# Column means of an 8192 × 8192 matrix: longer load runs, and three slabs folded on TensorE instead of one

## The chip, the cores and the metric

The kernel runs on one core of a Trainium2 chip. The metric is the device time of the kernel in microseconds, the median of several runs. One execution was also taken with the hardware profiler; its "span" runs from its first to its last instruction.

## The reference

```python
x = np.random.randn(8192, 8192).astype(np.float32)
def reference(x):
    return np.mean(x, axis=0)
```

So 268.4 MB are read, each element is added once into one of 8192 column sums, and 8192 floats are written.

## The kernel before

A **slab** is 128 rows, one row on each of the 128 partitions of the on-chip memory (SBUF); in float32 a slab is 4.19 MB and one row 32 KB. There are 64 slabs. They are loaded mostly two at a time, a **pair**: a partition gets two rows, 16384 elements, in one of three buffers `bufs[0..2]` (L48). Since a column sum doesn't depend on which row lands on which partition, rows are handed out so that each partition reads long contiguous runs of memory: `blocks` (L73) gives each partition RUN = 7 consecutive rows per block, so that a partition's rows start 7 × 32 KB = 224 KB after those of the partition before it. `source` (L78) takes three pairs from each block, as runs of 64 KB, and the seventh rows that are left over (`single`, L75) make pairs 27 to 30 and slab 62, as runs of 32 KB at most. The last slab, 63, is the last 128 rows of `x`, a partition's row 32 KB after that of the partition before.

`cuts` (L85) says into how many loads a pair is split: pair 0 into two (its first 2048 columns, then the rest), pairs 1 to 24 into one, pairs 25 to 29 into two rows of 8192 columns, pair 30 into four half rows. Slab 62 comes in two halves (L161), the last slab in eight pieces (L165): four wide ones of 2048, 2048, 2048 and 1408 columns, and four narrow ones of 192, 288, 96 and 64. All loads but pair 0's are issued by SyncE (SP) in this order, and SP's queue is in order: a load that waits holds up those behind it. The load of pair k waits until pair k − 3's buffer is free, which is when VectorE (DVE) has done the first add of pair k − 2 (L149 to L151); slab 62 and the pieces of the last slab share the buffer of pair 28 and wait in the same way, for the first add of pair 29 (L162).

**DVE** does nearly all of the summing. With the running sum in the first half of one buffer, each pair takes two adds of 8192 columns: `new[0:C] += old[0:C]` (frees the old buffer), then `new[0:C] += new[C:2C]`. Pairs 1 to 24 are done in a loop of eight turns (L181, LOOPED = 24), the others by a written-out list `adds` (L116 to L134), one add for each load, each waiting for its own load: two adds per pair for 25 to 29, four adds of 4096 columns for pair 30, and four of 2048 columns that add slab 62 to the running sum, `total`.

**TensorE (PE)** sums over the partitions: a matmul with a 128 × 32 matrix of ones as the stationary operand adds up 128 partitions of up to 512 columns into a bank of PSUM. `fold_wide` (L207) does a wide piece with four such matmuls, one to each quarter of the array's columns; `fold_narrow` (L215) does a narrow piece with one. Each matmul is two records in the trace, so a wide fold is eight. PE folds `total` piece by piece as DVE finishes it (`open_wide`, L234), and each piece of the last slab on top of it as that lands (`close`, L226), in an order written out at L239 to L256. Ahead of that, it does four matmuls on an unused tile `idle` (L240).

**The end**: ScalarE (ACT) drains wide pieces 0 to 2 from PSUM, times 1/8192, DVE drains wide piece 3, and both share the narrow ones (`drain`, L263). Four stores follow, three on SP and the last on ACT (L314 to L319).

Of the kernel before, what the change touches and what calls it, by code (L numbers as in the profile page):

```python
# [7 lines left out]
F32 = mybir.dt.float32  # L8
ADD = mybir.AluOpType.add
MULT = mybir.AluOpType.mult  # L10
P = 128
# [3 lines left out]
WIDE = (2048, 2048, 2048, 1408)  # L15
NARROW = (192, 288, 96, 64)
PIECES = WIDE + NARROW
FIRST = 2048
BY_ROW = 6
RUN = 7  # L20
LOOPED = 24


@with_exitstack
def kernel(
# [5 lines left out]
    nc = tc.nc  # L31
    R, C = x.shape
    n_slabs = R // P
    n_pairs = n_slabs // 2 - 1
    N0 = sum(WIDE)
    H = C // 2
    assert n_slabs % 2 == 0 and N0 + sum(NARROW) == sum(PIECES) == C
    assert LOOPED % 3 == 0 and LOOPED < n_pairs - 1
    inv_r = 1.0 / float(R)

    const_pool = ctx.enter_context(tc.tile_pool(name="const", bufs=1))
    psum_pool = ctx.enter_context(
        tc.tile_pool(name="acc", bufs=1, space=bass.MemoryType.PSUM)
    )
    res_pool = ctx.enter_context(tc.tile_pool(name="res", bufs=1))

    ones = const_pool.tile([P, 32], F32, name="ones")
    bufs = [nc.alloc_sbuf_tensor(f"pair{b}", [P, 2 * C], F32, align_bytes=512).ap() for b in range(3)]  # L48
    banks = [psum_pool.tile([P, 512], F32, name=f"bank{b}", tag=f"bank{b}") for b in range(8)]
    rw = nc.alloc_sbuf_tensor("rw", [P, 3 * 512], F32).ap()  # L50
    r3 = nc.alloc_sbuf_tensor("r3", [P, WIDE[3] // GROUPS], F32).ap()
    row = nc.alloc_sbuf_tensor("row", [P, C - N0], F32).ap()[0:1, :]
    idle = res_pool.tile([P, 512], F32, name="idle")

    wide, lo = [], 0
    for n, w in enumerate(WIDE):
# [2 lines left out]
    narrow = []  # L59
    for n, w in enumerate(NARROW):  # L60

        at = NARROW[2] if n == 3 else 0
        narrow.append((lo, w, 32 * min(n, 2), banks[4 + min(n, 2)], at))
        lo += w
    ending = (narrow[2][0], sum(NARROW[2:]), narrow[2][2], narrow[2][3], 0)

    n_blocks = (R - P) // (P * RUN)
    n_whole = n_blocks * (RUN // 2)  # L70
    assert R == (n_blocks * RUN + 1) * P and 2 * n_whole + n_blocks == 2 * n_pairs + 1
    assert LOOPED < n_whole
    blocks = x[0 : R - P, :].rearrange("(b p j) c -> b p (j c)", p=P, j=RUN)  # L73

    def single(n, lo, hi):  # L75
        return blocks[n, :, (RUN - 1) * C + lo : (RUN - 1) * C + hi]

    def source(k, lo, hi):  # L78
        if k < n_whole:
            b, t = divmod(k, RUN // 2)  # L80
            return blocks[b, :, 2 * t * C + lo : 2 * t * C + hi]
        j = lo // C
        return single(2 * (k - n_whole) + j, lo - j * C, hi - j * C)

    def cuts(k):  # L85
        if k == 0:
            return [(0, FIRST), (FIRST, 2 * C)]
        if k < n_pairs - BY_ROW:
            return [(0, 2 * C)]
        step = H if k == n_pairs - 1 else C  # L90
        return [(lo, lo + step) for lo in range(0, 2 * C, step)]

    def untracked(ap, size):

# [5 lines left out]


    early = nc.scalar.dma_start(out=untracked(bufs[0][:, 0:FIRST], 2 * C * P), in_=source(0, 0, FIRST))  # L102
    early.then_inc(first, 16)
    tc.no_tile_sem_insts.add(early.ins.name)
# [4 lines left out]
    with tc.tile_critical(sync_engine=mybir.EngineType.Pool) as section:  # L109
        tc.declare_no_dep(section, early.ins, reason="awaited by first")  # L110
        freed, half = sem("freed"), sem("half")
        dve, act, pe = sem("dve"), sem("act"), sem("pe")
        came = {}


        adds, freed_by = [], {}  # L116
        for k in range(LOOPED + 1, n_pairs):
            pair, before = bufs[k % 3], bufs[(k - 1) % 3]
            pieces = cuts(k)
            for n, (lo, hi) in enumerate(pieces):  # L120
                if lo < C:
                    adds.append(((k, n), pair[:, lo:hi], before[:, lo:hi]))
                else:
                    adds.append(((k, n), pair[:, lo - C : hi - C], pair[:, lo:hi]))
                if hi == C:
                    freed_by[k - 1] = len(adds)
        total = bufs[(n_pairs - 1) % 3]
        slab = bufs[n_pairs % 3][:, 0:C]
        last = bufs[n_pairs % 3][:, C : 2 * C]
        parts = [(lo, lo + 2048) for lo in range(0, C, 2048)]  # L130
        done = []
        for lo, hi in parts:
            adds.append((("slab", lo // H), total[:, lo:hi], slab[:, lo:hi]))
            done.append(len(adds))  # L134


        def load(key, dst, src, after=None):

            ld = (nc.scalar if key[0] == 0 else nc.sync).dma_start(out=dst, in_=src)  # L139
            if after is not None:  # L140
                ld.wait_op(after[0], after[1], "sem-ge")
            if key not in came:
                came[key] = sem(f"came_{'_'.join(map(str, key))}")
            ld.then_inc(came[key], 16)

        for k in range(n_pairs):
            for n, (lo, hi) in enumerate(cuts(k)):
                after = None
                if k >= 3 and n == 0:  # L149
                    f = k - 3  # L150
                    after = (freed, f + 1) if f < LOOPED else (dve, freed_by[f])  # L151
                if k == 1:
                    after = (first, 16)
                key = (k, n)
                if k <= LOOPED:
                    came[key] = first if (k, n) == (0, 0) else landed[k % 3]
                if key == (0, 0):
                    continue
                load(key, bufs[k % 3][:, lo:hi], source(k, lo, hi), after)
        r = (n_slabs - 2) * P  # L160
        for n in range(2):  # L161
            after = (dve, freed_by[n_pairs - 3]) if n == 0 else None  # L162
            load(("slab", n), slab[:, n * H : n * H + H], single(n_blocks - 1, n * H, n * H + H), after)
        at, lo = {}, 0
        for n, w in enumerate(PIECES):  # L165
            load(("last", n), last[:, lo : lo + w], x[r + P : R, lo : lo + w])
            for c in range(lo, lo + w, 32):
                at[c] = came["last", n]
            lo += w


# [1 line left out]
            return nc.vector.tensor_tensor(out=a, in0=a, in1=b, op=ADD)  # L173

        nc.vector.memset(ones, 1.0)  # L175
        nc.vector.memset(idle, 0.0)  # L176
        nc.vector.wait_ge(first, 16)
        vadd(bufs[0][:, 0:C], bufs[0][:, C : 2 * C]).wait_op(landed[0], 16, "sem-ge").then_inc(landed[0], -16)
        with nc.vector.register("left") as left:
            nc.vector.reg_mov(left, LOOPED // 3)  # L180
            with nc.vector.While(lambda: nc.vector.snap(left) > 0):  # L181
# [22 lines left out]
        def mm(dst, src, **flags):  # L204
            return nc.tensor.matmul(out=dst, lhsT=ones, rhs=src, skip_group_check=True, **flags)  # L205

        def fold_wide(n, src, **flags):  # L207
            lo, w, bank = wide[n]
            q = w // GROUPS
            for g in range(GROUPS):  # L210
                a = lo + g * q
                m = mm(bank[32 * g : 32 * g + 32, 0:q], src[:, a : a + q], **flags)
            return m

        def fold_narrow(part, src, **flags):  # L215
            lo, w, g, bank, at = part
            return mm(bank[g : g + 32, at : at + w], src[:, lo : lo + w], **flags)
# [3 lines left out]
        def landed_at(lo):  # L221
            if at[lo].num not in waited:
                waited.add(at[lo].num)
                nc.tensor.wait_ge(at[lo], 16)

        def close(fold, n, lo):  # L226
            nonlocal n_pe
            landed_at(lo)
            fold(n, last, start=False, stop=n != narrow[2]).then_inc(pe, 1)
            n_pe += 1  # L230
            return n_pe

        ready = {}
        def open_wide(n):  # L234
            nc.tensor.wait_ge(dve, done[n])
            fold_wide(n, total, start=True, stop=False)


        nc.tensor.wait_ge(dve, done[0] - 2)  # L239
        for _ in range(4):  # L240
            nc.tensor.matmul(  # L241
                out=banks[7][:, 0:512], lhsT=idle[:, 0:P], rhs=idle, start=True, stop=True, skip_group_check=True
            )
        open_wide(0)
        open_wide(1)
        ready["wide", 0] = close(fold_wide, 0, wide[0][0])
        open_wide(2)
        ready["wide", 1] = close(fold_wide, 1, wide[1][0])
        nc.tensor.wait_ge(dve, done[3])
        fold_wide(3, total, start=True, stop=False)  # L250
        for part in (*narrow[:2], ending):
            fold_narrow(part, total, start=True, stop=False)
        ready["wide", 2] = close(fold_wide, 2, wide[2][0])
        ready["wide", 3] = close(fold_wide, 3, wide[3][0])
        for n in range(len(narrow)):
            ready["narrow", n] = close(fold_narrow, narrow[n], narrow[n][0])  # L256

# [19 lines left out]
        for n, (engine, part) in enumerate(  # L277
            ((nc.scalar, narrow[0]), (nc.vector, narrow[1]), (nc.scalar, ending))
        ):
            lo, w, g, bank, _ = part  # L280
# [69 lines left out]
```

## Time and profile before

| what | value |
|---|---|
| median of 3 runs | 627.12 us (626.93 to 627.29) |
| the profiled execution, and its span | 627.51 us, 625.7 us |
| PE busy | 13.6 us, 86 matmul records |
| DVE busy | 541.3 us, 71 instructions |
| ACT busy | 3.7 us |
| HBM read over the span | 268.44 MB, 429 GB/s |
| DVE add of 8192 / 4096 / 2048 columns | 8.69 / 4.42 / 2.29 us, ×59 / ×4 / ×4 |
| PE: matmul records of 512 / 352 columns with `ones` | ×48 / ×16 |
| loads issued by SP | 48 |
| a whole pair's load, from issue to landing | 29.8 us (median of 24) |

How to read the profile: the page's slices cut the span into 40 equal parts of 15.6 us and show each engine's busy share in tenths, the TensorE clock granted, and what the 16 DMA engines moved. The chain of waits starts at the last instruction and goes back at each step to what released it; here it is read in order of time, one line per step, with start and duration in us, and "issue" for time in which nothing that the profile shows was waited for. The timeline has one line per stretch of like instructions (start, duration, engine, line, operation, output and input, count), with the idle time before it and its releaser in brackets. SPq and ACTq are the queues of DMA issues, PEld the loads of PE's stationary operand. L173 is every DVE add, L205 every matmul with `ones`, L139 every load.

### The profile page before, as it was taken

What the parts mean: (1) busy time and instruction counts of PE and PEld (TensorE: products, weight loads), DVE (VectorE), ACT (ScalarE), POOL (GpSimd) and SP (SyncE); (2) the same over time, 40 slices, a digit from 0 to 9 for tenths busy, and PEclk for the clock granted to TensorE, in tenths of its full rate; (3) what the DMA queues carried; (4) which work ended last, traced back from release to release, by engine and by line L of the source; (5) the groups of instructions that cost most, each with busy time, mean ns of one, the idle gap of its engine ahead of it and who ended that gap; (6) DMA issues with size and microseconds to landing.
All of it is one profiled execution on the core that took longest, in us unless ns stands there. A gap on an engine that the chain in (4) does not pass through costs nothing.

```text
span 625.7 us, 475 instructions
## 1 busy us (share of the span) xinstructions
PE 13.6 (2%) x86; PEld 4.6 (1%) x86; DVE 541.3 (87%) x71; ACT 3.7 (1%) x6; POOL 0.2 (0%) x4
## 2 busy tenths in 40 slices
PE   0000000000000000000000000000000000000025
PEld 0000000000000000000000000000000000000011
DVE  0049999989888899888898888988889899999996
ACT  0000000000000000000000000000000000000001
POOL 0000000000000000000000000000000000000000
PEclk9999999999999999999999999999999999999999
DMA  9999999999999999999999999999999999999997
GB/s 377 436 461 402 469 402 469 402 469 402 469 402 469 402 432 440 402 469 402 469 402 469 402 469 402 469 402 469 402 465 406 432 425 419 434 436 436 434 422 320
DMA packets 7231, 268.48 MB, mean 429 GB/s; under 512 B 1069, under 2 KB 1329, under 8 KB 1470
## 3 DMA queue, kind: packets, MB, share of 16 engines
q1 hardware_dynamic: 6940, 260.08, 96.2%
q10 hardware_dynamic: 290, 8.39, 3.2%
q14 instruction: 1, 0.01, 0.0%
HBM read 268.44 MB, written 0.03 MB: 429 GB/s over the span
## 4 chain that ended last, share of the span: by engine, by line
DMA 59%; DVE 39%; issue 0%; SPq 0%; DVEq 0%; PE 0%; ACTq 0%
DMA pair<-in_x_dram 59%; DVE pair L173 39%; SPq L139 0%; PE bank L205 0%; DVE r L269 0%; DVEq L109 0%; ACTq L102 0%; DVEq L186 0%; DVEq L184 0%; DVEq L173 0%; ACTq L345 0%
## 5 line engine op out<-in xcount | busy, mean ns | idle before, releaser
L173 DVE TENSOR_TENSOR pair<-pair 128x8192 f32<-128x8192 f32 (+2 forms) x67 | 539.7, 8056 | 78.0 <-DMA pair<-in_x_dram 73.7
L241 PE MATMUL bank<-idle 128*128 128x512 f32 x8 | 5.3, 817 | 605.6 <-DVE pair L173 605.6
L205 PE MATMUL bank<-pair,ones 128*32 128x512 f32 (+5 forms) x78 | 8.4, 523 | 3.8 <-DVE pair L173 3.6
L241 PEld LDWEIGHTS bank<-idle 128*128 128x128 f32 x8 | 2.1, 276 | 607.9 <-DVE pair L173 605.6
L266 ACT ACTIVATE rw<-bank 128x512 f32<-128x512 f32 x3 | 1.8, 597 | 617.3 <-PE bank L205 617.3
L269 DVE TENSOR_SCALAR r<-bank 128x352 f32<-128x352 f32 x1 | 0.5, 525 | 3.2 <-PE bank L205 3.2
L205 PEld LDWEIGHTS bank<-pair,ones 128*32 128x32 f32 x78 | 2.5, 108 | 10.2 <-DVE pair L173 7.1
L266 ACT ACT_TABLE_LOAD x1 | 1.3, 1283 | 1.8 <-issue 1.8
L175 DVE MEMSET ones<- 128x32 f32 x1 | 0.1, 85 | 1.0 <-PEq L334 1.0
L266 ACT ACTIVATE row<-bank 1x192 f32<-1x192 f32 (+1 forms) x2 | 0.6, 308 | 0.7 <-PE bank L205 0.7
L176 DVE MEMSET idle<- 128x512 f32 x1 | 0.5, 485 | 0.1
L269 DVE TENSOR_SCALAR row<-bank 1x288 f32<-1x288 f32 x1 | 0.4, 448 | 0.0
L334 POOL MEMSET const-bfloat16-1.0<- 128x1 bf16 x1 | 0.1, 101 | 0.0
L334 POOL MEMSET const-uint8-127<- 128x1 uint8 x1 | 0.1, 101 | 0.0
L334 POOL MEMSET const-float32-0.0<- 128x1 f32 x1 | 0.1, 98 | 0.2 <-issue 0.2
L334 POOL MEMSET const-float32-1.0<- 128x1 f32 x1 | 0.1, 98 | 0.0
## 6 DMA issues: line engine op xcount, KB each, us to landing
pair<-in_x_dram SPq DMA_DIRECT2D x10, 4096.0 KB, 27.6
pair<-in_x_dram SPq DMA_DIRECT2D x6, 2048.0 KB, 28.4
pair<-in_x_dram ACTq DMA_DIRECT2D x1, 7168.0 KB, 37.9
pair<-in_x_dram SPq DMA_DIRECT2D x3, 1024.0 KB, 33.4
pair<-in_x_dram ACTq DMA_DIRECT2D x1, 1024.0 KB, 4.7
pair<-in_x_dram SPq DMA_DIRECT2D x1, 704.0 KB, 36.6
pair<-in_x_dram SPq DMA_DIRECT2D x24, 29.8
pair<-in_x_dram SPq DMA_DIRECT2D x1, 144.0 KB, 30.2
```

Of the source, the lines that this page charges most:

```text
L173: return nc.vector.tensor_tensor(out=a, in0=a, in1=b, op=ADD)
L175: nc.vector.memset(ones, 1.0)
L176: nc.vector.memset(idle, 0.0)
L205: return nc.tensor.matmul(out=dst, lhsT=ones, rhs=src, skip_group_check=True, **flags)
L241: nc.tensor.matmul(out=banks[7][:, 0:512], lhsT=idle[:, 0:P], rhs=idle, start=True, stop=True, skip_group_check=True)
L266: op = engine.mul(out=dst, in_=src, mul=inv_r).then_inc(act, 1)
L269: op = engine.tensor_scalar(out=dst, in0=src, scalar1=inv_r, scalar2=None, op0=MULT).then_inc(dve, 1)
L334: nc = _bacc.Bacc("TRN2", target_bir_lowering=False, num_devices=1)
```

## The change

RUN becomes 6: a block gives each partition six consecutive rows, 192 KB apart from partition to partition, and three pairs in 64 KB runs with no row left over. Ten blocks make pairs 0 to 29; pair 30 is the next 256 rows (`two`), and slab 62 and the last slab together are the final 256 rows (`end`), two consecutive rows to a partition, so 64 KB apart. Every pair but pair 0 is one load. Slab 62 and the first 2048 columns of the last slab lie side by side both in memory and in the buffer, and come in one load of 40 KB runs; the other seven pieces of the last slab are loaded as before. DVE's loop covers 27 pairs; pairs 28 and 29 are written out. Pair 30 isn't added to the running sum any more: DVE adds its two slabs to each other, 2048 columns at a time. PE folds four things into each bank: the running sum, pair 30's sum, slab 62, and the last slab. The four matmuls on `idle` and the tile itself are gone.

```diff
-BY_ROW = 6
-RUN = 7
-LOOPED = 24
+RUN = 6
+LOOPED = 27
...
+    per_block = RUN // 2
+    n_blocks = (n_pairs - 1) // per_block
+    R0 = n_blocks * RUN * P
+    blocks = x[0:R0, :].rearrange("(b p j) c -> b p (j c)", p=P, j=RUN)
+    two = x[R0 : R0 + 2 * P, :].rearrange("(p j) c -> p (j c)", j=2)
+    end = x[R0 + 2 * P : R, :].rearrange("(p j) c -> p (j c)", j=2)
...
     def source(k, lo, hi):
-        if k < n_whole:
-            b, t = divmod(k, RUN // 2)
-            return blocks[b, :, 2 * t * C + lo : 2 * t * C + hi]
-        j = lo // C
-        return single(2 * (k - n_whole) + j, lo - j * C, hi - j * C)
+        if k == n_pairs - 1:
+            return two[:, lo:hi]
+        b, t = divmod(k, per_block)
+        return blocks[b, :, 2 * t * C + lo : 2 * t * C + hi]
 
     def cuts(k):
-        if k == 0:
-            return [(0, FIRST), (FIRST, 2 * C)]
-        if k < n_pairs - BY_ROW:
-            return [(0, 2 * C)]
-        step = H if k == n_pairs - 1 else C
-        return [(lo, lo + step) for lo in range(0, 2 * C, step)]
+        return [(0, FIRST), (FIRST, 2 * C)] if k == 0 else [(0, 2 * C)]
...
+        for k in range(LOOPED + 1, n_pairs - 1):
             pair, before = bufs[k % 3], bufs[(k - 1) % 3]
+            adds.append(((k, 0), pair[:, 0:C], before[:, 0:C]))
+            freed_by[k - 1] = len(adds)
+            adds.append(((k, 0), pair[:, 0:C], pair[:, C : 2 * C]))
+        n_total = len(adds)
+        total = bufs[(n_pairs - 2) % 3]
+        pair = bufs[(n_pairs - 1) % 3]
...
-            adds.append((("slab", lo // H), total[:, lo:hi], slab[:, lo:hi]))
+            adds.append(((n_pairs - 1, 0), pair[:, lo : lo + 2048], pair[:, C + lo : C + lo + 2048]))
             done.append(len(adds))
...
+        final = bufs[n_pairs % 3]
+        load(("slab", 0), final[:, 0 : C + WIDE[0]], end[:, 0 : C + WIDE[0]], (dve, freed_by[n_pairs - 3]))
         for n, w in enumerate(PIECES):
+            key = ("last", n) if n else ("slab", 0)
+            if n:
+                load(key, final[:, C + lo : C + lo + w], end[:, C + lo : C + lo + w])
...
+        def fold_all(src, **flags):
+            for n in range(len(wide)):
+                fold_wide(n, src, **flags)
+            for part in (*narrow[:2], ending):
+                fold_narrow(part, src, **flags)
+
+        nc.tensor.wait_ge(dve, n_total)
+        fold_all(total, start=True, stop=False)
+        for n in range(len(wide)):
             nc.tensor.wait_ge(dve, done[n])
-            fold_wide(n, total, start=True, stop=False)
...
+            fold_wide(n, pair, start=False, stop=False)
         for part in (*narrow[:2], ending):
+            fold_narrow(part, pair, start=False, stop=False)
+        landed_at(0)
+        fold_all(slab, start=False, stop=False)
+        for n in range(len(wide)):
+            ready["wide", n] = close(fold_wide, n, wide[n][0])
         for n in range(len(narrow)):
             ready["narrow", n] = close(fold_narrow, narrow[n], narrow[n][0])
```

More of the change, by code (lines that the diff above doesn't have):

```diff
@@ L35 @@
     N0 = sum(WIDE)
-    H = C // 2
     assert n_slabs % 2 == 0 and N0 + sum(NARROW) == sum(PIECES) == C
-    assert LOOPED % 3 == 0 and LOOPED < n_pairs - 1
+    assert LOOPED % 3 == 0 and LOOPED < n_pairs - 2
     inv_r = 1.0 / float(R)
@@ L44 @@
     )
-    res_pool = ctx.enter_context(tc.tile_pool(name="res", bufs=1))
     ones = const_pool.tile([P, 32], F32, name="ones")
@@ L52 @@
     row = nc.alloc_sbuf_tensor("row", [P, C - N0], F32).ap()[0:1, :]
-    idle = res_pool.tile([P, 512], F32, name="idle")
     wide, lo = [], 0
@@ L65 @@
     ending = (narrow[2][0], sum(NARROW[2:]), narrow[2][2], narrow[2][3], 0)
[L69 to L76, printed above, removed]
-    def source(k, lo, hi):
-        if k < n_whole:
-            b, t = divmod(k, RUN // 2)
-            return blocks[b, :, 2 * t * C + lo : 2 * t * C + hi]
-        j = lo // C
-        return single(2 * (k - n_whole) + j, lo - j * C, hi - j * C)
-    def cuts(k):
-        if k == 0:
-            return [(0, FIRST), (FIRST, 2 * C)]
-        if k < n_pairs - BY_ROW:
-            return [(0, 2 * C)]
-        step = H if k == n_pairs - 1 else C
-        return [(lo, lo + step) for lo in range(0, 2 * C, step)]
+    per_block = RUN // 2
+    n_blocks = (n_pairs - 1) // per_block
+    R0 = n_blocks * RUN * P
+    assert n_blocks * per_block == n_pairs - 1 and R == R0 + 4 * P
+    blocks = x[0:R0, :].rearrange("(b p j) c -> b p (j c)", p=P, j=RUN)
+    two = x[R0 : R0 + 2 * P, :].rearrange("(p j) c -> p (j c)", j=2)
+    end = x[R0 + 2 * P : R, :].rearrange("(p j) c -> p (j c)", j=2)
+    def source(k, lo, hi):
+        if k == n_pairs - 1:
+            return two[:, lo:hi]
+        b, t = divmod(k, per_block)
+        return blocks[b, :, 2 * t * C + lo : 2 * t * C + hi]
+    def cuts(k):
+        return [(0, FIRST), (FIRST, 2 * C)] if k == 0 else [(0, 2 * C)]
     def untracked(ap, size):
@@ L116 @@
         adds, freed_by = [], {}
-        for k in range(LOOPED + 1, n_pairs):
+        for k in range(LOOPED + 1, n_pairs - 1):
             pair, before = bufs[k % 3], bufs[(k - 1) % 3]
[L119 to L127, printed above, removed]
+            adds.append(((k, 0), pair[:, 0:C], before[:, 0:C]))
[4 more added lines that the diff above has]
+        pair = bufs[(n_pairs - 1) % 3]
         slab = bufs[n_pairs % 3][:, 0:C]
         last = bufs[n_pairs % 3][:, C : 2 * C]
-        parts = [(lo, lo + 2048) for lo in range(0, C, 2048)]
         done = []
-        for lo, hi in parts:
-            adds.append((("slab", lo // H), total[:, lo:hi], slab[:, lo:hi]))
+        for lo in range(0, C, 2048):
+            adds.append(((n_pairs - 1, 0), pair[:, lo : lo + 2048], pair[:, C + lo : C + lo + 2048]))
             done.append(len(adds))
@@ L159 @@
                 load(key, bufs[k % 3][:, lo:hi], source(k, lo, hi), after)
[L160 to L163, printed above, removed]
+        final = bufs[n_pairs % 3]
+        load(("slab", 0), final[:, 0 : C + WIDE[0]], end[:, 0 : C + WIDE[0]], (dve, freed_by[n_pairs - 3]))
         at, lo = {}, 0
         for n, w in enumerate(PIECES):
-            load(("last", n), last[:, lo : lo + w], x[r + P : R, lo : lo + w])
+            key = ("last", n) if n else ("slab", 0)
+            if n:
+                load(key, final[:, C + lo : C + lo + w], end[:, C + lo : C + lo + w])
             for c in range(lo, lo + w, 32):
-                at[c] = came["last", n]
+                at[c] = came[key]
             lo += w
@@ L175 @@
         nc.vector.memset(ones, 1.0)
-        nc.vector.memset(idle, 0.0)
         nc.vector.wait_ge(first, 16)
@@ L233 @@
         ready = {}
-        def open_wide(n):
-            nc.tensor.wait_ge(dve, done[n])
-            fold_wide(n, total, start=True, stop=False)
[L239 to L250, printed above, removed]
-        for part in (*narrow[:2], ending):
-            fold_narrow(part, total, start=True, stop=False)
-        ready["wide", 2] = close(fold_wide, 2, wide[2][0])
-        ready["wide", 3] = close(fold_wide, 3, wide[3][0])
+        def fold_all(src, **flags):
[6 more added lines that the diff above has]
+        for n in range(len(wide)):
+            nc.tensor.wait_ge(dve, done[n])
+            fold_wide(n, pair, start=False, stop=False)
+        for part in (*narrow[:2], ending):
+            fold_narrow(part, pair, start=False, stop=False)
[3 more added lines that the diff above has]
+            ready["wide", n] = close(fold_wide, n, wide[n][0])
         for n in range(len(narrow)):
```

## The prediction

> **What bounds the kernel now.** I read the page's slices first, then the chain of waits in order of time, then the timeline of the last 45 us. The first view says which resource never rests.
>
> ```profile
> DVE  0049999989888899888898888988889899999996
> DMA  9999999999999999999999999999999999999997
> GB/s 377 436 461 402 469 402 469 402 469 402 469 402 469 402 432 440 402 469 402 469 402 469 402 469 402 469 402 469 402 465 406 432 425 419 434 436 436 434 422 320
> ```
>
> The DMA engines are busy in every slice. The swing between 469 and 402 GB/s is no swing in speed: a packet of 64 KB lasts about 2.4 us, and a slice of 15.6 us counts the ends of six or of seven of them on 16 engines. So rates must come from landings, which the chain gives:
>
> ```profile
> 138.51 0.03 issue
> ...
> 486.54 0.03 issue
> ...
> 585.00 36.62 DMA pair<-in_x_dram
> 621.63 0.04 issue
> 621.67 0.84 PE bank L205 x8
> 622.52 0.02 issue
> 622.54 0.53 DVE r L269
> 623.07 0.48 DVEq L109
> ```
>
> The waits that end at 138.51 and 486.54 are landings of pair 6 and pair 24, whole pairs of 8.389 MB (by counting: each pair has two adds on DVE). 348.03 us for 18 pairs is **19.335 us a pair, 433.9 GB/s**. After pair 24 DVE stays a bit behind until it waits 0.77 us before 583.48 (next fence), which is the landing of the second row of pair 29, about 583.43. And at 621.63 wide piece 3 of the last slab lands; the end of the chain follows it. So the transfers bound the kernel from the first to the last microsecond, and what follows the landing at 621.63 (PE 0.84, DVE 0.53, the last store) is the tail.
>
> ```profile
> 583.48 35.84 DVE L173 TENSOR_TENSOR pair<-pair 128x8192 f32<-128x8192 f32 x9 [0.77 <-DMA pair<-in_x_dram]
> 606.62 0.34 PEld L241 LDWEIGHTS bank<-idle 128*128 128x128 f32 x1 [0.52 <-issue]
> 607.47 0.34 PEld L241 LDWEIGHTS bank<-idle 128*128 128x128 f32 x1 [0.52 <-issue]
> 608.32 0.34 PEld L241 LDWEIGHTS bank<-idle 128*128 128x128 f32 x1 [0.52 <-issue]
> 608.98 0.19 PEld L241 LDWEIGHTS bank<-idle 128*128 128x128 f32 x1 [0.32 <-issue]
> 609.41 0.19 PEld L241 LDWEIGHTS bank<-idle 128*128 128x128 f32 x1 [0.24 <-issue]
> 612.39 1.06 PE L205 MATMUL bank<-pair,ones 128*32 128x512 f32 x8 [1.53 <-DVE pair L173]
> 617.04 1.92 PE L205 MATMUL bank<-pair,ones 128*32 128x512 f32 x16 [0.40 <-DVE pair L173]
> 619.37 2.13 PE L205 MATMUL bank<-pair,ones 128*32 128x352 f32 x22 [0.40 <-DVE pair L173]
> 621.67 1.32 PE L205 MATMUL bank<-pair,ones 128*32 128x352 f32 x16 [0.18 <-DMA pair<-in_x_dram]
> ```
>
> DVE ends its adds at 619.32, PE ends the fold that follows at 621.50, and the landing comes at 621.63: three engines finish within a hair of each other, but the landing is last.
>
> **Prices from these rows.** One fold of a wide piece (8 records): 1.06 us alone, 1.92 for two, so 0.86 each in a row and 0.20 for the last to drain. The row at 619.37 holds wide 3, three narrow folds and one wide close: 2.13 − 1.06 = 1.07 for wide 3 with the narrow ones. A slab folded whole is then 3 × 0.86 + 1.07 = **3.65 us**. DVE adds: 8.69 us for 8192 columns, 4.42 for 4096, 2.29 for 2048 (groups by shape).
>
> **Part 1: longer runs, fewer loads.** SP issues 48 loads now, 38 after: pairs 25 to 29 five fewer, pair 30 three, slab 62 with the first piece of the last slab two. What does a load cost beyond its bytes? Pairs 25 to 29, in rows of 32 KB and two loads each, took 583.43 − 486.54 = 96.89 us against 5 × 19.335 = 96.68: 0.21 us for five extra loads. From 583.43 to 621.63 came 16.449 MB (four slabs less 640 columns) in 38.20 us; at 433.9 GB/s it would be 37.91: 0.29 us for ten loads where two would be the least. Both say **about 0.04 us per extra load**, run length included. Ten fewer: −0.4 us. The bounds: nothing (landings are read to some tenths, and a DVE wait shows only the last one), and −1.5 us, if I went instead by the bytes counted in windows: 422 GB/s over 583.4 to 622.1 and 432 over 486.5 to 583.4 against 434 of the steady part, 1.1 + 0.4 us. I take 0.4, since the counted bytes depend on which packets end inside the window.
>
> **Part 2: does the transfer ever starve?** A pair's load waits for the first add of two pairs before, so it is issued 8.7 us after a landing, with 10.6 us of the next pair still to come. The loop's three more turns, and pairs 28 and 29 behind it, keep that pattern. The 40 KB load waits for the first add of pair 29, and pair 30 is moving meanwhile. Seven pieces queue behind it on SP at 0.33 to 0.43 us an issue (the chain's SPq steps before 585.00), some 3.5 us of the 10.6. SP's last issues of now, up to 4.22 us each, are held up by loads still queued; with nine in place of eighteen behind pair 29 that can only shrink. Nothing else is on SP before the stores. Cost: nothing; without that cover it would be the delay itself, us for us.
>
> **Part 3: DVE.** It loses four adds of 4096 columns (17.7 us, off the path) and keeps 59 of 8192 and four of 2048. It now waits for whole pairs again. By the 64 KB pace pair 29 lands at 583.2, its two adds end at 600.7, pair 30 lands at 602.6, and its four pieces are done at 604.9, 607.2, 609.5 and 611.8. The two memsets at the start become one, 0.48 us under a wait of 37.7: nothing.
>
> **Part 4: PE.** The four idle matmuls (5.26 us) go; two folds of whole slabs come. The sum: running total from 600.7, slow at first. The idle matmuls show why: their weight loads stand 0.85 us apart until 608.3 and 0.43 from 609.0, while the page's PEclk stays at 9 throughout, so I go by the spacing. With 3.4 us at half speed, 3.65 becomes 5.35: done at 606.1. Pair 30's first piece waits for nothing then, the others for DVE: the last ends at 611.8 + 1.07 + 0.20 = 613.1. The 40 KB load (5.243 MB, 12.1 us) lands at 614.7; PE has waited 1.6 us. From there slab 62 and the closes of wide 0, 1, 2: 3.65 + 3 × 0.86 = 6.23 us. Wide 3 lands 5504 columns after the 40 KB load, 2.818 MB: 6.50 us, and some 0.1 for three loads. **PE is ready 0.3 us before the landing that already set the end**: cost nothing. Behind it everything is as now: close of wide 3, narrow closes, DVE's drain, the last store. The first store leaves about 1.6 us later than now, at 621, and the second near 622; the third waits for DVE's drain as before.
>
> **Sum.** −0.4 us on the profiled execution's 627.51 (span 625.7 and 1.8 around it): 627.1. The median shown is 0.39 under that execution, so the forecast is 627.12 − 0.4 = **626.7**. A measurement of this kernel tells 0.2% from no change, 1.25 us: I forecast no difference, for the transfers' bytes are the same and they already run at the pace of the long runs.
>
> **The rivals.**
> - *PE late.* The fold of slab 62 moves behind the 40 KB landing, 3.65 us that DVE did ahead of it before. The slack is 0.3 us. If PE runs at half speed there, for 3.4 us, 6.23 becomes 7.93: 1.3 us late, 628.0. If it stays slow throughout, 12.5 us for the chain and 0.7 more for the last close: 633. For: the matmuls at 605.60 that brought it to speed are gone, and PE idles 1.6 us just before. Against: in this trace PE idled 1.53 us before 612.39, was then busy 1.06 of 2.33 us, and its next folds still took 0.86 each; and the running total's fold gives over 5 us of work. Chance 0.05 for the first, 0.04 for the second. The Trainium skill, TensorE: Matmul & The Clock Gate, "What's actually happening", says that the half rate returns after at least one idle window of about 3.4 us and that the windows run free. The gaps here stay under one window, so by that rule PE stays fast; the trace agrees for 1.53 us, and nothing here shows a longer gap after a start.
> - *The other addresses are slower.* This is the rival for the slower side: the place is every load, as partitions are 192 KB apart in memory instead of 224, and 64 KB in the last two groups instead of 224 and 32. The only stretch with another distance (the last slab, 32 KB) lies in the 38.2 us that ran 0.8% under the pace, which I put down to loads. If addresses did that, and the new ones cost 0.8% over all 580 us behind the start, it is +4.6: 631.3. It decides from a loss of 0.3%, 1.7 us. Against: 224 KB and 32 KB apart differ by less than 1%. Chance 0.10. The Trainium skill, DMA: Bandwidth & Descriptors, "Latency and other measured facts", reports copies slowed by row distances of large powers of two, from 512 KiB up (207 for 214 GB/s); by that scale 64 KB and 192 KB should lose nothing, and no run so far shows such a distance.
> - *Nothing is saved*, a load's end being hidden behind the next, or PE eats it: 627.1 to 627.5. For: the engines never rest. Chance 0.15.
> - *More is saved*, the 1.5 us of the counted bytes: 625.6. Chance 0.08.
> - The forecast, 626.4 to 627.0: 0.58.
>
> Within 0.2% lie the forecast, nothing saved, and the short slow PE: 0.78. Faster is 0.08; slower is 0.10 + 0.04 = 0.14. The range holds all but the slower cases, 625.5 to 628.8.
>
> **What would show it.** Right: pair landings still 19.3 us apart to the end, whatever the distance; DVE done near 612; PE's chain from 614.7 in one stretch of some 6.2 us, and a short wait before wide 3; the last landing at 621.1 to 621.4. Wrong: landings further apart than 19.4 (addresses), PE's eight-record folds 1.7 us apart behind the 40 KB landing or no wait before wide 3 (PE late), a gap in the DMA row near 602 or 614 (a load issued too late).

## The result, and the profile after

The changed kernel takes **628.20 us** (median of 22 runs, 627.83 to 628.68), beside 627.35 us for the kernel before (22 runs on the same chips). The ratio is 1.0014, 95% interval 1.0008 to 1.0020: 0.85 us slower, where I forecast 0.4 us faster. It lies within the 0.2% that I called no difference and inside my range, but on the other side of 1, and with 22 runs the sign is sure. The profiled execution's span is 626.6 us, 0.9 over the one before.

The end of the chain of waits of the changed kernel, in order of time (start, duration, what):

```profile
583.22 0.03 issue
...
593.36 29.16 DMA pair<-in_x_dram
622.52 0.04 issue
622.57 0.84 PE bank L191 x8
623.41 0.02 issue
623.43 0.52 DVE r L251
623.96 0.48 DVEq L99
```

It reads as before: the end follows the landing of wide piece 3, now at 622.52 in place of 621.63. Pair 29 landed at 583.22, where I had 583.2. So nothing was lost before, and 1.3 us against my 621.2 was lost in the last 39 us. The timeline of that stretch says where not to look:

```profile
600.79 8.11 PE L191 MATMUL bank<-pair,ones 128*32 128x512 f32 x54 [600.79 <-DVE pair L160]
602.68 9.27 DVE L160 TENSOR_TENSOR pair<-pair 128x2048 f32<-128x2048 f32 x4 [1.95 <-DMA pair<-in_x_dram]
612.00 1.27 PE L191 MATMUL bank<-pair,ones 128*32 128x352 f32 x14 [1.26 <-DVE pair L160]
614.72 5.56 PE L191 MATMUL bank<-pair,ones 128*32 128x512 f32 x54 [1.44 <-DMA pair<-in_x_dram]
620.87 1.06 PE L191 MATMUL bank<-pair,ones 128*32 128x512 f32 x8 [0.59 <-DMA pair<-in_x_dram]
622.57 1.29 PE L191 MATMUL bank<-pair,ones 128*32 128x352 f32 x16 [0.64 <-DMA pair<-in_x_dram]
```

Pair 30 lands at 602.6 and the 40 KB load at 614.7, both to 0.1 us as worked out, and PE's folds behind it run at full pace (54 records in 5.56 us). But PE then waits twice for a landing: wide 2 is there at 620.82, not at 619.5. A load is spread over 16 DMA engines, and the trace has a time for each of its 16 completions (it doesn't name the engine); the chain shows only the last. For wide 2, in us from the span's start:

```
                 first   8th     15th    16th
before           619.50  619.62  619.83  619.91
changed          619.15  619.30  619.54  620.82
```

Fifteen engines are 0.3 us *earlier* than before, as forecast. **One engine is 1.28 us behind the other fifteen**, and in every piece after, one completion is again 1.2 to 1.3 us behind; I take it for the same engine. A piece has landed when its last engine has. What else the DMA engines carried stands in the page's list of DMA queues (queue and kind, packets, MB, share):

```profile
q1 hardware_dynamic: 5500, 260.08, 96.0%
q10 hardware_dynamic: 290, 8.39, 3.2%
q8 instruction: 1, 0.02, 0.0%
```

The page of before has no `q8` row, only `q14 instruction: 1, 0.01`, a packet at 624.86 us, behind all loads. The changed kernel's packet on q8 is 16384 bytes, starts at 618.34 us and lasts 0.94 us by the trace: one packet, hence one engine, though the trace doesn't say which. The theory this suggests, **the code theory**: PE's program has grown from 172 to 308 records of weight loads and matmuls; while PE runs through it, a further 16 KB block of it is fetched, through one of the engines that carry the last slab. The Trainium skill, Runtime: NRT & Kernel Launch, "Instruction fetch mechanics", says that an engine's instructions are refilled in blocks of 16 KiB, 256 instructions, by the sequencer's own DMA queue. The packet's size agrees; the Trainium skill calls the cost there mostly hidden, and the runs below put it at 1.1 to 1.3 us here. The main rival, **the address theory**: 8 KB runs that lie 64 KB apart are slow on one engine. A third would be that PE's folds themselves are late.

### The profile page after: what moved, and what is told of

It reads as the page before. It is cut to its first block, busy times and chain, and to the rows that moved or that the text cites. A ratio compares the mean times of both kernels' runs of the same rounds, so it can differ in the third digit from the quotient of the medians.

```text
span 626.6 us, 594 instructions
## 1 busy us (share of the span) xinstructions
PE 18.4 (3%) x154; PEld 6.0 (1%) x154; DVE 523.1 (83%) x66; ACT 3.7 (1%) x6; POOL 0.2 (0%) x4
## 4 chain that ended last, share of the span: by engine, by line
DMA 72%; DVE 26%; issue 0%; DVEq 0%; SPq 0%; PE 0%; ACTq 0%
DMA pair<-in_x_dram 72%; DVE pair L160 26%; SPq L126 0%; PE bank L191 0%; DVE r L251 0%; DVEq L99 0%; DVEq L172 0%; ACTq L92 0%; DVEq L170 0%; DVEq L160 0%; ACTq L327 0%; DVEq L180 0%
## 5 line engine op out<-in xcount | busy, mean ns | idle before, releaser
L160 DVE TENSOR_TENSOR pair<-pair 128x8192 f32<-128x8192 f32 (+1 forms) x63 | 522.0, 8286 | 88.9 <-DMA pair<-in_x_dram 84.6
L191 PE MATMUL bank<-pair,ones 128*32 128x512 f32 (+5 forms) x154 | 18.4, 597 | 605.5 <-DVE pair L160 602.8
L191 PEld LDWEIGHTS bank<-pair,ones 128*32 128x32 f32 x154 | 6.0, 120 | 617.7 <-DVE pair L160 604.9
```

## The experiments

Each kernel was timed 11 times, beside 33 runs of the kernel before on the same chip (their median is 627.21 us for the first four kernels and for the last four). "Records" are PE's weight loads and matmuls; "late" is the 16th engine's landing of wide 3 behind the 15th's.

| run | records | time, us | ratio to before (95%) | 16 KB packet at | wide 3 landed | late |
|---|---|---|---|---|---|---|
| e1_no_slab62 | 232 | 628.54 | 1.0020 (1.0011 to 1.0029) | 620.35 | 622.37 | 1.62 |
| e2_old_last_addresses | 308 | 628.14 | 1.0015 (1.0006 to 1.0024) | 615.98 | 622.29 | 1.26 |
| e3_before_more_code | 308 | 628.55 | 1.0019 (1.0010 to 1.0028) | 617.91 | 622.70 | 1.32 |
| e4_before_code_at_start | 420 | 628.27 | 1.0015 (1.0006 to 1.0024) | 11.68 | 622.54 | 0.47 |
| e5_short_code | 172 | 626.83 | 0.9994 (0.9985 to 1.0003) | none | 620.95 | 0.10 |
| e6_short_code_more_loads | 172 | 628.30 | 1.0017 (1.0008 to 1.0026) | none | 621.91 | 0.10 |
| e7_after_two_fetches | 556 | 628.53 | 1.0021 (1.0012 to 1.0030) | 11.65, 618.97 | 622.31 | 0.28 |
| e8_before_little_code | 192 | 627.34 | 1.0004 (0.9995 to 1.0014) | 626.09 | 621.36 | 0.03 |

**e1_no_slab62**: less code, by leaving slab 62 out of the sums.

```diff
         landed_at(0)
-        fold_all(slab, start=False, stop=False)
```

> The changed kernel without the 19 matmuls that fold slab 62 on PE (slab 62 is left out of the sums; all loads are as in the changed kernel). PE then runs 58 matmuls, 232 records, in place of 308; the single 16 KB instruction packet of the changed kernel started when 238 records had begun. Code theory (that packet holds up one of the 16 DMA engines for 1.28 us and with it the last landings): the packet comes after the data or not at all, the spread of wide piece 2's 16 landings falls from 1.67 us to 0.4, wide 3 lands at 621.2 to 621.4 and the time is 1.2 to 1.3 us under the changed kernel, 626.9 to 627.0, 0.4 under the kernel before. Address theory (8 KB runs that lie 64 KB apart are slow on one engine): nothing changes in the loads, 628.2, wide 3 at 622.5. PE theory (the fold of slab 62 sets the end): a gain only if PE now waits longer, and the landings as in the changed kernel.

The expectation failed, twice. The packet came all the same, 2.0 us later and with 200 records begun, and hit wide 3 instead of wide 2: 232 records are still too many, so I had the limit wrong. And PE got slow. The windows of this run (stretch, its length, busy time and count of PE, PEld, DVE, ACT and POOL, then PE's granted clock, DMA share, GB/s):

```profile
612.00:614.00 2.00, 1.82 (x14) 0.38 (x6) 0.00 (x0) 0.00 (x0) 0.00 (x0) 0.50 1.01 434
618.00:620.00 2.00, 0.91 (x8) 0.16 (x8) 0.00 (x0) 0.35 (x1) 0.00 (x0) 1.00 1.00 417
...
622.00:623.00 1.00, 0.58 (x4) 0.20 (x8) 0.00 (x0) 0.00 (x0) 0.00 (x0) 0.50 0.07 21
623.00:624.00 1.00, 1.00 (x14) 0.60 (x8) 0.12 (x1) 0.00 (x0) 0.00 (x0) 0.50 0.00 0
```

The granted clock is 0.50 at 612 and again from 622 on; in the profiled execution of the changed kernel it is 1.00 in all these stretches. The folds show the same in their own lines of the timeline:

```profile
611.47 2.35 PE L191 MATMUL bank<-pair,ones 128*32 128x352 f32 x14 [1.26 <-DVE pair L160]
...
619.09 1.07 PE L191 MATMUL bank<-pair,ones 128*32 128x512 f32 x8 [1.40 <-DMA pair<-in_x_dram]
622.41 2.35 PE L191 MATMUL bank<-pair,ones 128*32 128x352 f32 x16 [2.26 <-DMA pair<-in_x_dram]
```

The same 16 records took 1.29 us in the changed kernel, so 1.06 us of this execution's end are PE at half speed (from the landing of wide 3 to the end of the span it is 4.98 us, in the changed kernel 4.08). Of the 11 times four lie at 627.9 and five at 629.1 to 629.5; the profiled execution is one of the upper kind. The granted clock, averaged over the whole execution, is 0.994 to 0.997 in the lower four and 0.990 to 0.993 in the upper five. That the code sets the end is not shown by this run; that the fold of slab 62 does not, is: without it the landings are as late.

**e2_old_last_addresses**: slab 62 and the last slab with rows 32 KB apart from partition to partition, with PE's matmuls unchanged. The last slab had that distance in the kernel before; slab 62 had 224 KB there.

```diff
-        load(("slab", 0), final[:, 0 : C + WIDE[0]], end[:, 0 : C + WIDE[0]], (dve, freed_by[n_pairs - 3]))
+        load(("slab", 0), slab, x[r : r + P, :], (dve, freed_by[n_pairs - 3]))
...
+            load(key, last[:, lo : lo + w], x[r + P : R, lo : lo + w])
...
-        landed_at(0)
+        nc.tensor.wait_ge(came["slab", 0], 16)
```

> The changed kernel with slab 62 and the last slab taken as 128 rows each, 32 KB apart from partition to partition as in the kernel before, slab 62 in one load and all eight pieces of the last slab in loads of their own (39 loads on SP). PE's program is unchanged. Code theory: the instruction packet is still there, one landing of wide 2 or wide 3 is 1.3 us behind the other 15, 628.2. Address theory: all 16 landings within 0.4 us again, wide 3 at 621.3, 627.0.

The code theory's number came, 628.14. With rows 32 KB apart one engine is still late, 1.31 us in wide 1, behind a packet that now starts at 615.98. The address theory falls.

**e3_before_more_code**: only code, in the kernel before.

```diff
+        nc.tensor.wait_ge(dve, done[0] - 4)
+        for _ in range(34):
+            nc.tensor.matmul(
+                out=banks[7][0:32, 0:8], lhsT=ones, rhs=ones[:, 0:8], start=True, stop=True, skip_group_check=True
+            )
         nc.tensor.wait_ge(dve, done[0] - 2)
```

> The kernel before with 34 tiny matmuls (8 columns, into an unused PSUM bank) ahead of its four idle ones, about 596 us into the span, so that PE has 308 records like the changed kernel. Nothing waits for them. Code theory: a 16 KB instruction packet at about 618 us, one engine's landings 1.3 us late from there on, 627.35 + 1.28 = 628.6. Address theory, and any theory that puts the loss on loads or folds of the changed kernel: 627.35, no change.

As the code theory said, 628.55 against 628.6. The loads, the addresses and DVE are those of before; the queue list of its page gains one row beside that of before:

```profile
q1 hardware_dynamic: 6940, 260.08, 96.0%
q10 hardware_dynamic: 290, 8.39, 3.2%
q8 instruction: 1, 0.02, 0.0%
q14 instruction: 1, 0.01, 0.0%
```

Fifteen engines bring wide 2 by 619.71, the last at 621.00, and PE, which in the kernel before went from one fold to the next, waits for it:

```profile
619.17 1.27 PE L205 MATMUL bank<-pair,ones 128*32 128x352 f32 x14 [0.40 <-DVE pair L173]
621.05 1.06 PE L205 MATMUL bank<-pair,ones 128*32 128x512 f32 x8 [0.61 <-DMA pair<-in_x_dram]
622.75 1.29 PE L205 MATMUL bank<-pair,ones 128*32 128x352 f32 x16 [0.64 <-DMA pair<-in_x_dram]
```

The last two of these lines are those of the changed kernel to 0.2 us: the whole signature of the loss, made by instructions whose results nothing uses.

**e4_before_code_at_start**: the same loss early, with 62 tiny matmuls that wait only for the matrix of ones.

```diff
-        nc.vector.memset(ones, 1.0)
+        lit = sem("lit")
+        nc.vector.memset(ones, 1.0).then_inc(lit, 1)
...
+        nc.tensor.wait_ge(lit, 1)
+        for _ in range(62):
+            nc.tensor.matmul(
+                out=banks[7][0:32, 0:8], lhsT=ones, rhs=ones[:, 0:8], start=True, stop=True, skip_group_check=True
+            )
         nc.tensor.wait_ge(dve, done[0] - 2)
```

> The kernel before with 62 tiny matmuls at the very start of PE's program, so that PE passes the same number of records (about 238) a few us into the span and not again. If an engine's lost time is never made up, because its queue is never empty: 628.6 as in the run with the code late, and one landing out of 16 is 1.3 us behind the others in every load of the stretch. If it is made up on the way: 627.35, landings within 0.4 us. I expect the first, at 0.6. Address theory: 627.35.

628.27, +1.06: the time lost at 11.68 us is still missing 610 us later. One engine is 1.19 to 1.22 us behind in loads two to four. The detail I did not expect: from the fifth load on two engines are behind, by some 0.95 and 1.4 us, to the end (wide 3: fourteen by 621.12, then 622.07 and 622.54). Why a second engine shares it is open.

**e5_short_code**: the changed kernel's loads with 172 records. It leaves out the folds of the running total and of pair 30's sum.

```diff
+    idle = const_pool.tile([P, 512], F32, name="idle")
...
+        nc.vector.memset(idle, 0.0)
...
-        nc.tensor.wait_ge(dve, n_total)
-        fold_all(total, start=True, stop=False)
...
+        nc.tensor.wait_ge(dve, done[1])
+        for _ in range(4):
+            nc.tensor.matmul(
+                out=banks[7][:, 0:512], lhsT=idle[:, 0:P], rhs=idle, start=True, stop=True, skip_group_check=True
+            )
         landed_at(0)
-        fold_all(slab, start=False, stop=False)
+        fold_all(slab, start=True, stop=False)
```

> The changed kernel with PE's program cut to the length of the kernel before (172 records): the folds of the running total and of pair 30's sum are left out (so only the last two slabs are in the output; DVE's adds and all loads are unchanged), and four matmuls on a zero tile bring PE up to speed before the 40 KB load lands. From 614.7 on PE does what the changed kernel does. Code theory: no 16 KB packet before the last landing, the 16 landings of each piece within 0.4 us, wide 3 at 621.2, and the time 1.3 under the changed kernel and 0.4 under the kernel before: 626.8. Had the saving by fewer loads been a mistake of mine: 627.2.

626.83 against 626.8. Its page has no instruction row at all, and all 16 engines are within 0.4 us of each other:

```profile
q1 hardware_dynamic: 5500, 260.08, 96.1%
q10 hardware_dynamic: 290, 8.39, 3.2%
HBM read 268.44 MB, written 0.03 MB: 430 GB/s over the span
```

Its chain ends as my prediction drew the changed kernel's:

```profile
593.02 27.93 DMA pair<-in_x_dram
620.95 0.04 issue
620.99 0.84 PE bank L193 x8
```

This is 0.38 us under the kernel before, which is my −0.4; its own interval reaches from −0.0015 to +0.0003 and so doesn't exclude no gain. Against the changed kernel, each beside its own runs of the kernel before, it is 0.85 + 0.38 = 1.2 us; the two intervals (0.5 to 1.3 us over, and 0.9 under to 0.2 over) don't overlap.

**e6_short_code_more_loads**: that run with 27 loads more.

```diff
-        return [(0, FIRST), (FIRST, 2 * C)] if k == 0 else [(0, 2 * C)]
+        if k == 0:
+            return [(0, FIRST), (FIRST, 2 * C)]
+        return [(0, C), (C, 2 * C)] if k <= LOOPED else [(0, 2 * C)]
...
-                    nc.vector.wait_ge(landed[new], 16)
+                    nc.vector.wait_ge(landed[new], 32)
```

> The run with the short code, with each of pairs 1 to 27 in two loads of 32 KB runs, 27 loads more. At 0.04 us a load it is 1.1 us longer than that run, 627.9; if loads cost nothing, the same; at the price from the counted bytes (some 0.1 us each) 2.7 us longer.

+1.47 us, more than the 1.1 expected. The landing of wide 3 moves by 0.96 us, from 620.95 to 621.91, which is **0.036 us per extra load**, run length included: my price. This is one trace against one, and traces of the same loads differ too (wide 3 landed at 621.63 in the kernel before, at 621.36 in e8), so the price is known to about a third. The other 0.5 us lies behind the landing of the last store (1.32 us from there to the end of the span, 0.82 in the short-code run and in the changed kernel). What it is, is open; if it belonged to the loads, the price would be 0.054.

**e7_after_two_fetches**: the 62 tiny matmuls at the start of the changed kernel.

```diff
-        nc.vector.memset(ones, 1.0)
+        lit = sem("lit")
+        nc.vector.memset(ones, 1.0).then_inc(lit, 1)
...
+        nc.tensor.wait_ge(lit, 1)
+        for _ in range(62):
+            nc.tensor.matmul(
+                out=banks[7][0:32, 0:8], lhsT=ones, rhs=ones[:, 0:8], start=True, stop=True, skip_group_check=True
+            )
         nc.tensor.wait_ge(dve, n_total)
```

> The changed kernel with 62 tiny matmuls at the very start of PE's program, so that a first 16 KB packet comes near 11 us and a second near 618. If both hold up the same DMA engine and nothing is made up, the last landing is 1.1 to 1.3 us later than in the changed kernel, 629.3 to 629.5. If they fall on different engines, no more than the changed kernel, 628.2.

Two packets, as foreseen:

```profile
q1 hardware_dynamic: 5500, 260.08, 95.9%
q10 hardware_dynamic: 290, 8.39, 3.2%
q8 instruction: 2, 0.03, 0.0%
```

But the delays don't add: wide 3 is late against the other thirteen (620.87 at the latest) by 0.65, 1.16 and 1.44 us on three engines (621.52, 622.03, 622.31), and lands 0.2 us before the changed kernel's. Wide 2, ahead of the second packet's effect, had two engines late, by 0.66 and 1.24 us; so the second packet fell on an engine other than the latest one. The time, 628.53, is neither 628.2 nor 629.3, and its 11 values spread from 628.06 to 629.06. The three executions with a mean granted clock of 1.000 took 628.17 to 628.25, as expected for different engines; all six from 628.53 up have 0.995 to 0.997, so PE at half speed may be what lengthened them, which their times alone don't show. The run decides the landings, not the time.

**e8_before_little_code**: the kernel before with 5 tiny matmuls, where e3 had 34 (192 records).

```diff
+        nc.tensor.wait_ge(dve, done[0] - 4)
+        for _ in range(5):
+            nc.tensor.matmul(
+                out=banks[7][0:32, 0:8], lhsT=ones, rhs=ones[:, 0:8], start=True, stop=True, skip_group_check=True
+            )
         nc.tensor.wait_ge(dve, done[0] - 2)
```

> The kernel before with 5 tiny matmuls, 192 records in all. In the runs so far the 16 KB packet started with 194 to 238 records begun. Code theory: what counts is where PE's program passes a block, so the packet comes behind the last landing or not at all, 627.2, no change. If it is any added PE instruction that costs: 0.2 us for a seventh of the 34 of the earlier run.

627.34, no change that can be told; the interval holds 0.2 us as well as none, so the time alone doesn't decide. The landings do: the packet comes at 626.09, behind the end of the span (625.6), and no engine is late. So it is not PE's extra work but the block of code, and only when it is fetched while loads run. (The expectation's "194 to 238 records begun" leaves out e4, where 248 had begun.)

## Why the prediction was wrong, step by step

- **What bounds the kernel, part 1 (loads), part 2 (starving), part 3 (DVE): right.** Pairs land 19.3 us apart at either distance; the landings of pair 29, pair 30 and the 40 KB load are 583.22, 602.59 and 614.67 (forecast 583.2, 602.6, 614.7). DVE is done at 611.95 (611.8). The saving by ten fewer loads is 0.38 us where nothing else interferes (e5), at 0.036 us a load by landings (e6).
- **Part 4 (PE): its time had room enough, the conclusion failed.** The running total's fold took until 607.2 where I had 606.1: its weight loads stand 0.85 us apart up to 605.91, so the slow start lasted 5.2 us and not 3.4. Nothing waited for that. The chain behind the 40 KB load took 5.56 us up to the close of wide 1, and PE was ready for wide 2 at 620.28. The step that failed is the sentence "PE is ready 0.3 us before the landing that already set the end: cost nothing". It priced 34 more matmuls as engine time under a cover, and took the landing as given. Their instructions are themselves a transfer: a 16 KB packet on one of the 16 engines whose slowest sets that landing. Missing term: +1.1 to 1.3 us (1.28 in the landings; with the code alone 1.34 in e3 and 1.06 in e4). −0.4 + 1.28 = +0.88; measured +0.85.
- **"Nothing else is on SP before the stores" (part 2)** was true and too narrow: I listed what queues on SP, not what else uses the DMA engines. (My "eighteen" loads behind pair 29 were fourteen; nothing rests on it.) The page of before shows that kind of packet, in its list of queues, and I didn't ask what calls it up.
- **The rivals.** *Addresses*: the sign came, the mechanism did not (e2). *PE late*: not the cause. Ten of the changed kernel's 22 executions have a mean granted clock of 1.000, and their median is 628.08; the other twelve have 0.995 to 0.997 and 628.2. But my reason against it, the short gaps, was no reason (last section). *More is saved*: e5's interval, −0.9 to +0.2 us, leaves 1.5 out. None of my rivals was the cause, and the chances that I gave to "slower" rested on two mechanisms that weren't the one at work. That my range held 628.20 is luck: no term of mine stood for the packet.
- **What would show it.** I had named a short wait before wide 3 as the sign of being right. The wait was there, 0.64 us, but it was the sign of the loss.

## What to carry to other kernels

Where the DMA engines never rest, an idle engine's instructions are not free: count them, not only their time, and look at the page's instruction packets before adding work to an engine; here 192 records of PE were still free and 232 were not. A load has landed only with the last of its 16 completions, so one packet on one engine delayed the whole load, and in these runs, whose queues had no slack, the delay was not made up, whether the packet came at 12 us or at 618; two packets on different engines (e7) didn't add up. When a landing is late, compare the 16 completions before suspecting the addresses. The saving by fewer loads is some 0.04 us each, for ten of them a third of what the code cost; none of these runs points to a complete version that is clearly faster than the kernel before.

## What the runs showed of the hardware that I had not expected

One 16 KB instruction packet of 0.93 to 0.97 us set its engine back by 1.2 to 1.3 us (1.28 in the changed kernel, 1.31 in e2, 1.29 in e3; 1.62 where it fell among 5.6 KB runs in e1).

PE's clock fell to half without a long gap. In e2 it was down from 611.46 to 614.87 us, with no gap above 1.26 us just before; the windows view gives

```profile
608.05:611.46 3.41, 1.15 (x12) 0.16 (x8) 3.38 (x2) 0.00 (x0) 0.00 (x0) 1.00 0.80 344
...
611.50:614.80 3.30, 3.08 (x23) 1.75 (x27) 0.16 (x1) 0.00 (x0) 0.00 (x0) 0.50 1.00 422
615.00:616.00 1.00, 1.00 (x14) 0.72 (x10) 0.00 (x0) 0.00 (x0) 0.00 (x0) 1.00 1.00 418
```

The clock changes at steps of 3.41 us or multiples of it: in the trace of e1 it is full for 6.83 us, half for 3.41 and full for 6.83, in e2 6.83, 3.41 and 10.24. It fell behind steps in which PE was busy 1.06, 1.07 (e1), 1.15 (e2, the first line) and 1.29 us (e2, at the end), with no idle piece inside them above 1.55 us, and held behind steps of 1.75 (e1), 1.85 (the changed kernel), 1.96 (the one before) and more. So a step that is two thirds idle, in pieces, is enough; the Trainium skill, TensorE: Matmul & The Clock Gate, "What's actually happening", speaks of an idle window of about 3.4 us: the length agrees, but it needn't be idle throughout. In e2 the slow stretch cost nothing, in e1 a second one cost 1.06 us. My rival "PE late" had its condition wrong: in these traces it is the busy share of a step that decides, not the longest gap (a step with an idle piece of 1.44 us held in the changed kernel, one with none above 1.26 fell in e2). Its price of 1.3 us is not shown by any run; at the last closes, where I had 0.7 us, e1 shows 1.06.
